# Output projection of a Griffin-style block: five pairs of token tiles as seven block products each

## The chip, the cores and the metric

The kernel runs on one core of one Trainium2 chip. The metric is the device time of one execution in microseconds; the kernel before takes 2026.76 us (median of 3 runs, 2026.57 to 2026.84).

A core has five engines that run side by side, each with a queue of its own: TensorE (PE, matmul; its weight loads are shown apart as PEld), VectorE (DVE), ScalarE (ACT), GpSimd (POOL) and SyncE (SP), which here only issues DMA transfers. An engine takes its instructions in the order of its queue. An instruction that must wait holds back those behind it.

## The reference

One encoder layer over 2048 tokens of 1024 channels, all float32. Two attention branches, a and b, each give 512 channels per token; a gated merge and an output projection with a residual follow:

```python
merged = gate_a * (ya @ w_branch_a[layer]) + gate_b * (yb @ w_branch_b[layer])
h = h + merged @ w_out[layer]          # 2048x1024 @ 1024x1024
return rms_norm(h, final_norm_gain)    # each row divided by the root of its mean square, times a gain
```

The change is in the last two lines: the product with `w_out`, the sum with x, and the norm of each row.

## The kernel before

**Precision.** TensorE takes operands in a rounded float32 form. So each operand is kept as a high part (a rounded copy, made by ACT) and a low part (the rest: the value minus its high part, by DVE or POOL). This is called a split. A product of two operands is three matmuls: high x high, high x low, low x high (`mm3`, L225, and `product`, L1544).

**The stage ahead.** The attention of both branches is one long interleaved sequence. It writes the b branch's last result `y_of("b", 3)` late. `branch(m, G, c)` (L1081) multiplies a branch's result for 512 tokens (group G) with one of eight column blocks c of `w_branch`: it loads the weights (tag `dst`), splits them on ACT and POOL into the tile `dw` (L1087, L1088; one place for each), does 12 matmuls into the PSUM tile `d` (one place), multiplies by the gate on DVE (L1094, gate from tag `sig`), adds the other branch's part on POOL (L1101) and writes to `mD` in HBM. `mD[g]` is the merged result of 512 tokens, transposed: 128 x 8 blocks of channels x 512 tokens. When the last stage begins, only the eight `branch("b", 3, c)` are missing; they feed token tiles 12 to 15.

**The last stage** (L1519 to L1603) works on 16 token tiles of 128 rows. Their number is t. `load_m` (L1163) brings the merged result of a pair of tiles as four loads of 256 KB (tag `mf`) and splits each on ACT (L1170) and POOL (L1171) into one tile of `wp_` (tags P0 and P1 in turn). The eight weight blocks of 128 rows of `w_out` stand split on chip as `ws[k]`: blocks 0 to 4 (`wosh`, `wosl`, `wosy`) are prepared during attention, blocks 5 to 7 (`wos`) after its buffers are closed (L1145, L1146). Per tile and half of the 1024 output columns, `product` makes 8 x 3 matmuls of 128 tokens x 512 columns into one of four PSUM banks. DVE adds the row of x (L1594), ACT squares and sums (L1595). After both halves DVE takes the reciprocal root by whole-number arithmetic and three Newton steps in one column (`rsqrt`, L136 to L150) and multiplies by root and gain (L1602); SP writes the row out (L1603). Tile 15 (`last`) does the same with its last half cut in two.

**The order.** The kernel is written with a tile framework. It puts each engine's instructions into an order by a planner that runs a timeline of its own at compile time; waits are put in from the tiles' reads and writes. In the stage before the change the planner orders all engines: matmuls of `branch` stand between the matmuls of the tiles wherever its timeline found them ready. `tc.manual_schedule` takes an engine out of the planner's hands: that engine's instructions then stand in the order in which the program names them. A tile with a tag shares its place in memory with others of the tag, and its first writer waits until the readers of the one before are done.

## Time and profile before

| what | value |
|---|---|
| median of 3 runs | 2026.76 us |
| the profiled execution | 2026.53 us |
| its span | 2024.7 us |
| TensorE busy over the span | 1966.8 us (97%) |
| DVE, ACT, POOL busy over the span | 1446.5, 1268.4, 810.4 us |
| TensorE busy from 1840 to 1906 us | 65.99 of 66 us |
| TensorE busy from 1929 to 2011 us | 82.00 of 82 us |

The last stage takes the final 190 us of the span, from some matmuls before 1832 us that fill holes of the attention to the last row's way out. The lines of the profile name the engine, the line of the kernel, the operation, the tile it writes and the tiles it reads (`po<-wos,mm` writes the PSUM tile po from wos and mm), and in brackets how long the engine was idle before and what it waited for. A matmul's duration in the trace is its latency; matmuls overlap, so what one costs is the spacing of their starts.

### The profile page before, as it was taken

The page shows a single profiled execution, that of the slowest core. Times are in us where ns is not written, and L with a number is a line of the kernel's source. Part 1 is how long each engine was busy: PE and PEld are TensorE (multiplying, and loading weights), DVE is VectorE, ACT ScalarE, POOL GpSimd, SP SyncE. Part 2 cuts the span into 40 slices and gives each one's busy share as a digit, 9 for nine tenths or more (in the row PEclk, how much of TensorE's full clock was granted, in tenths as well). Part 3 has the DMA queues.
Part 4 walks back from the last instruction along what each step waited for, and adds up shares of the span by engine and source line. Part 5 has one row for each costly group of instructions (what it writes and reads, how often), then busy time and mean ns, then how long its engine had stood idle before and what let it go on. Part 6 is the DMA issues. An engine that isn't in the chain of part 4 may idle for free. (4 is left out here: it accounts for less than half of the span.)

```text
span 2024.7 us, 34050 instructions
## 1 busy us (share of the span) xinstructions
PE 1966.8 (97%) x10677; PEld 1685.8 (83%) x10677; DVE 1446.5 (71%) x3584; ACT 1268.4 (63%) x2539; POOL 810.4 (40%) x1057
## 2 busy tenths in 40 slices
PE   8999999999999999999989999999999999999998
PEld 7788888889889888778768888888988898887886
DVE  6737778797989988665556778658876688765444
ACT  6446666566576645355487879758986698773221
POOL 2232233321172454554335564563445444442420
PEclk9999999999999999999999999999999999999999
DMA  9573444565465665478998565574346531325632
GB/s 352 195 238 107 144 145 144 159 187 159 155 212 161 210 221 178 129 243 276 290 285 276 177 209 153 167 236 124 120 154 201 180 101 53 110 89 182 224 135 94
DMA packets 244730, 363.16 MB, mean 179 GB/s; under 512 B 31168, under 2 KB 115776, under 8 KB 244416
## 3 DMA queue, kind: packets, MB, share of 16 engines
q1 hardware_dynamic: 244544, 360.94, 55.4%
q8 instruction: 85, 1.39, 0.3%
q14 instruction: 101, 0.83, 0.1%
HBM read 244.23 MB, written 116.62 MB: 178 GB/s over the span
## 5 line engine op out<-in xcount | busy, mean ns | idle before, releaser
L225 PE MATMUL acc<-xh,wt 128*128 128x512 f32 x2128 | 676.6, 392 | 4.6 <-DVE keepikT L1476 1.3
L225 PEld LDWEIGHTS acc<-xh,wt 128*128 128x128 f32 x2128 | 399.4, 188 | 90.2 <-DVE wt L1291 1.9
L225 PE MATMUL acc<-xl,wt 128*128 128x512 f32 x1064 | 415.5, 391 | 0.1
L861 POOL TENSOR_TENSOR ptl<-pf,pth 128x512 fp32r<-128x512 f32 (+1 forms) x144 | 179.8, 1249 | 223.3 <-ACT pf L857 171.1
L225 PEld LDWEIGHTS acc<-xl,wt 128*128 128x128 f32 x1064 | 200.3, 188 | 41.2 <-DVE xl L1284 0.4
L864 DVE TENSOR_TENSOR ptl<-pt,pth 128x512 fp32r<-128x512 f32 (+1 forms) x288 | 187.1, 659 | 44.5 <-ACT pth L863 43.7
L515 DVE SCALAR_TENSOR_TENSOR sc<-lg,iw,sc 128x512 f32<-128x512 f32 (+2 forms) x266 | 178.7, 678 | 52.1 <-ACT lg L510 46.8
L216 POOL TENSOR_TENSOR wt<-wst,wt 128x512 fp32r<-128x512 f32 (+1 forms) x96 | 117.3, 1249 | 233.3 <-ACT wt L215 205.6
L1024 PE MATMUL s<-kBt,qsB 128*128 128x512 f32 (+3 forms) x640 | 188.8, 386 | 5.7 <-DVE mx L840 3.1
L510 ACT ACTIVATE lg<-lg 128x512 f32<-128x512 f32 (+2 forms) x304 | 150.2, 526 | 48.6 <-PE lg L508 47.5
L863 ACT ACTIVATE pth<-pt 128x512 fp32r<-128x512 f32 (+1 forms) x288 | 159.9, 579 | 33.1 <-PE pt L1041 16.7
L1027 ACT ACTIVATE P<-P,mx 128x128 f32<-128x128 f32 (+15 forms) x128 | 154.6, 1210 | 22.4 <-DVE mx L840 21.8
L1041 PE MATMUL pt<-ident,P 128*128 128x128 f32 x1088 | 166.6, 273 | 1.9 <-DVE ptl L864 0.8
L1049 PE MATMUL O<-pth,vBt 128*128 128x256 f32 x544 | 147.9, 290 | 3.5 <-ACT pth L863 1.5
L1049 PE MATMUL O<-ptl,vBt 128*128 128x256 f32 x544 | 147.3, 297 | 2.7 <-POOL ptl L861 1.3
L840 DVE CUSTOM_DVE_ANT_0 P<-s,mk,mx 128x512 f32<-128x512 f32 (+2 forms) x192 | 125.2, 652 | 29.4 <-PE s L1024 21.0
L1041 PEld LDWEIGHTS pt<-ident,P 128*128 128x128 f32 x1088 | 126.4, 140 | 11.3 <-DVE ptl L864 2.0
L1088 POOL TENSOR_TENSOR dw<-dst,dw 128x512 fp32r<-128x512 f32 x64 | 82.5, 1291 | 106.3 <-ACT dw L1087 99.5
L1024 PEld LDWEIGHTS s<-kBt,qsB 128*128 128x128 f32 x640 | 103.7, 192 | 18.7 <-DVE mx L840 9.7
L563 ACT ACTIVATE jk<-sc,st 128x640 int8<-128x640 f32 (+6 forms) x49 | 71.2, 1453 | 70.0 <-DVE st L581 60.4
L1049 PEld LDWEIGHTS O<-ptl,vBt 128*128 128x128 f32 x544 | 102.6, 189 | 12.8 <-DVE ptl L864 6.5
L914 PE MATMUL s<-kk,qz 128*128 128x256 f32 (+1 forms) x448 | 106.9, 334 | 5.5 <-DVE mx L840 5.2
(320 smaller groups left out, 4449.0 us busy)
## 6 DMA issues: line engine op xcount, KB each, us to landing
wst<-wP SPq DMA_DIRECT2D x80, 256.0 KB
wst<-wS SPq DMA_DIRECT2D x72, 256.0 KB
kk<-kA SPq DMA_DIRECT2D x56, 256.0 KB
vs<-vA SPq DMA_DIRECT2D x56, 256.0 KB
wst<-wS SPq DMA_DIRECT2D x72, 192.0 KB
qz<-qA SPq DMA_DIRECT2D x96, 128.0 KB
qD<-q SPq DMA_DIRECT2D x39, 256.0 KB
part<-qD SPq DMA_DIRECT2D x39, 256.0 KB
```

The costliest lines, as they stand in the source:

```text
L216: nc.gpsimd.tensor_tensor(wt[:, 1, k:k + n, c * 128:(c + 1) * 128], st, f32(hi), op=OP.subtract)
L225: m = nc.tensor.matmul(acc, a, b, start=(first and i == 0), stop=(last and i == n - 1), **({} if first and last else {"skip_group_check": ...
L510: nc.scalar.activation(lg, lg, AF.Relu)
L515: nc.vector.scalar_tensor_tensor(o_, lg, wv, o_, op0=OP.mult, op1=OP.add)
L840: nc.vector.tensor_tensor_reduce(dst, ps_, add, 1.0, FMAX if first else mx, OP.add, OP.min, accum_out=mx)
L861: nc.gpsimd.tensor_tensor(lo, pf, f32(hi), op=OP.subtract)
L863: nc.scalar.activation(hi, src, AF.Copy)
L864: nc.vector.tensor_tensor(lo, src, f32(hi), op=OP.subtract)
L1024: nc.tensor.matmul(s_ps[:, :w], q[:, h, :], kBt[:, m, a:a + w], start=(m == 0), stop=(m == 1))
L1027: nc.scalar.activation(P[:, e, :n], P[:, e, :n], AF.Exp, bias=mx[:, e:e + 1], scale=-1.0, accum_out=st["sum"][:, (u % 2) * 2 + e:(u % 2) * ...
L1041: nc.tensor.transpose(pt[:, k, e, :], P[:, e, (kt + k) * 128:(kt + k + 1) * 128], ident)
L1049: nc.tensor.matmul(o_, vBt[:, kt + k, :], src[:, k, :], start=(kt + k == 0 and n_ == 0), stop=(kt + k == b and n_ == 1), skip_group_check= ...
```

## The change

Tiles 0 to 5 (`FIRST7 = 6`) go as before. Tiles 6 to 15 go in five pairs. The operand of a pair is 256 tokens x 1024 channels. It is cut into four blocks A11, A12 (first tile, first and second half of the channels), A21, A22 (second tile); `w_out` into B11, B12, B21, B22 of 512 x 512. The 2 x 2 block product, eight block products of four k-steps, is now made with seven (Winograd's form of Strassen's method):

- operands, per pair: S1 = A21 + A22, S2 = S1 - A11, S3 = A11 - A21, S4 = A12 - S2;
- weights, once: T1 = B12 - B11, T2 = B22 - T1, T3 = B22 - B12, T4 = B21 - T2;
- products: A11 B11, A12 B21, S1 T1, S2 T2, S3 T3, A22 T4, S4 B22, put together by accumulating in PSUM and by additions on DVE and POOL with the rows of x.

The parts of the edit:

- Order: TensorE's queue in this stage is in the program's order. It begins with blocks 5 and 6 for the four half rows of tiles 0 and 1, then block 7; the eight `branch` products follow one per half row, from the second half of tile 1 to the first half of tile 5. Block 5 and 7 are staged over the tag `sig` (block 7 waits for block 5), no longer `dst`.
- `sums_of_weights(k)` after tiles 1 to 4, `last_sum_of_weights(k)` after tile 5: 12 and 4 loads of 256 KB, sums on POOL, splits on ACT and DVE. The first are held by a small copy on POOL from a value of the tile before. T4 lies in the places of the b branch's result (tags `yb0`, `yb1`), free after the last `branch`.
- `blocks(t)` loads a pair's operands (A1 in the place `dw`, 512 KB; A12 and A22 in `sig`), makes the four sums and seven splits; the splits of the next pair lie in a ring of eight places (P0, P1), and each is issued behind the product that frees its place.
- `seven(t, n, then)` is a pair; `close_pair` takes the roots of both rows at once, with its small values in a PSUM tile. The last pair makes A22 T4 in a bank of its own ahead of A12 B21, closes row 15 on POOL and ACT, and ends with tile 14's second half cut in two as before (`close_last`).

```diff
         for k in range(WK, KT):
             load_w(k, one_=wo.tile([128, 2, D], F32R, name=f"wos{k}"),
-                   tags=((("sig", 2), ("sig", 2)), (("dt", 2), ("dt", 2)), (("dst", 1), ("dst", 1)))[(KT - 1 - k) % 3])
+                   tags=((("sig", 2), ("sig", 2)), (("dt", 2), ("dt", 2)), (("sig", 2), ("sig", 2)))[k - WK])
...
+        def sums_of_weights(k, gate):
...
+            st = [ld.tile([128, 512], F32, name="tst", tag=g_, bufs=n) for g_, n in (("bias", 2), ("bias", 2), ("sg", SGB))]
+            for z, (k_, hf) in zip(st, ((k, 0), (k, 1), (k + 4, 1))):
+                nc.gpsimd.tensor_copy(z[:, 0:1], gate)
+                nc.sync.dma_start(z, io["wO"][:, k_, hf * 512:hf * 512 + 512])
+            nc.gpsimd.tensor_tensor(st[0], st[1], st[0], op=OP.subtract)
+            nc.gpsimd.tensor_tensor(st[1], st[2], st[1], op=OP.subtract)
+            nc.gpsimd.tensor_tensor(st[2], st[2], st[0], op=OP.subtract)
+            for j, z in ((1, st[0]), (3, st[1]), (2, st[2])):
+                nc.scalar.activation(twh[j][:, k], z, AF.Copy)
+                nc.vector.tensor_tensor(twl[j][:, k], z, f32(twh[j][:, k]), op=OP.subtract)
+
+        def last_sum_of_weights(k):
...
+            nc.sync.dma_start(z, io["wO"][:, k + 4, 0:512])
+            nc.gpsimd.tensor_tensor(z, z, f32(twh[2][:, k]), op=OP.subtract)
+            nc.gpsimd.tensor_tensor(z, z, f32(twl[2][:, k]), op=OP.subtract)
+            nc.scalar.activation(twh[4][:, k], z, AF.Copy)
+            nc.vector.tensor_tensor(twl[4][:, k], z, f32(twh[4][:, k]), op=OP.subtract)
+
+        def blocks(t):
...
+            A1 = dn.tile([128, 4, 256], F32, name="a1", tag="dw", bufs=1)
+            nc.sync.dma_start(A1, mD[g, :, 0:4, o:o + 256])
+            f = {"A11": A1[:, :, 0:128], "A21": A1[:, :, 128:256]}
+            for i in range(2):
+                f[f"A{i + 1}2"] = dn.tile([128, 4, 128], F32, name="a2", tag="sig")
+                nc.sync.dma_start(f[f"A{i + 1}2"], mD[g, :, 4:8, o + i * 128:o + i * 128 + 128])
...
+            def split(n_, e):
+                r_ = (rot("ring", 8) + 4) % 8
...
+                hi, lo = (ring[r_ // 4][:, r_ % 4, z] for z in range(2))
+                nc.scalar.activation(hi, f[n_], AF.Copy)
+                e.tensor_tensor(lo, f[n_], f32(hi), op=OP.subtract)
+                ops[t][n_] = hi, lo
+
+            split("A11", nc.vector)
+            for n_, tag, e, a, b, op in (("S1", "dt", nc.gpsimd, "A21", "A22", OP.add), ("S2", "dt", nc.vector, "S1", "A11", OP.subtract),
+                                         ("S3", "ta", nc.gpsimd, "A11", "A21", OP.subtract), ("S4", "ta", nc.vector, "A12", "S2", OP.subtract)):
...
+            for n_, e in (("S2", nc.vector), ("S1", nc.gpsimd), ("S3", nc.gpsimd), ("A12", nc.gpsimd), ("A22", nc.vector), ("S4", nc.gpsimd)):
+                yield
+                split(n_, e)
...
+        def close_pair(t, hs, ss):
+            z = psd.tile([128, 512], F32, name="rz", tag="d", bufs=1)
+            v, w, a = (z[:, 4 * i:4 * i + 2] for i in range(3))
...
+            for _ in range(NEWTON):
+                nc.vector.tensor_tensor(a, v, y, op=OP.mult)
+                nc.vector.tensor_tensor(a, a, y, op=OP.mult)
+                nc.vector.scalar_tensor_tensor(y, a, 1.5, y, op0=OP.add, op1=OP.mult)
+            for i in range(2):
+                for hf in range(2):
...
+                    nc.vector.scalar_tensor_tensor(hs[i][:, n_], hs[i][:, n_], y[:, i:i + 1], g2[:, n_], op0=OP.mult, op1=OP.mult)
+                nc.sync.dma_start(out[(t + i) * 128:(t + i + 1) * 128, :], hs[i])
+
+        def seven(t, n, then):
...
+            def times(acc, n_, w, first, last_):
+                block_product(acc, m[n_], w, first, last_)
+                if then:
+                    next(then, None)
...
+            times(a, "A11", bw(0, 0), True, False)
+            nc.scalar.activation(p1, a, AF.Copy)
+            nc.gpsimd.tensor_tensor(q12, p1, x0[:, v], op=OP.add)
+            nc.gpsimd.tensor_tensor(q22, p1, x1[:, v], op=OP.add)
+            nc.gpsimd.tensor_tensor(q21, p1, x1[:, u], op=OP.add)
+            times(b, "S2", tw(2), True, False)
+            nc.vector.tensor_tensor(q12, b, q12, op=OP.add)
+            times(c, "S1", tw(1), True, False)
+            times(b, "S3", tw(3), False, end)
+            nc.vector.tensor_tensor(q22, b, q22, op=OP.add)
+            nc.vector.tensor_tensor(h1[:, v], c, q22, op=OP.add)
...
+            times(a, "A12", bw(1, 0), False, True)
+            nc.vector.tensor_tensor(h0[:, u], a, x0[:, u], op=OP.add)
...
+            times(b, "A22", tw(4), False, True)
+            nc.vector.tensor_tensor(h1[:, u], b, q21, op=OP.add)
...
+            times(c, "S4", bw(1, 1), False, True)
+            nc.vector.tensor_tensor(h0[:, v], c, q12, op=OP.add)
...
+        ph.enter_context(tc.manual_schedule(engines={mybir.EngineType.PE}))
+        for t in range(2):
+            for hf in range(2):
+                product(t, hf, WK, KT - 1)
         load_r(0)
...
+        load_m(2)
+        c = 0
+        for t in range(FIRST7):
+            load_r(t + 1)
+            if t == 2:
+                load_m(4)
             for hf in range(2):
...
+                half_row(t, hf)
+                if (t > 1 or t and hf) and c < 8:
+                    branch("b", NG - 1, c)
+                    c += 1
+            if 1 <= t < 5:
+                sums_of_weights(t - 1, rows_[t - 1][1][:, 0:1])
+        for k in range(4):
+            last_sum_of_weights(k)
+        first = blocks(FIRST7)
+        for _ in first:
+            pass
+        load_r(FIRST7 + 1)
+        for n, t in enumerate(range(FIRST7, NT, 2)):
+            seven(t, n, blocks(t + 2) if t + 2 < NT else None)
...
```

More of the change, by code (lines that the diff above doesn't have):

```diff
@@ L63 @@
 FADE = 0.8
+FIRST7 = 6
 WIDE = 0.8
@@ L1531, in load_r, with cols_of, product @@
             nc.sync.dma_start(xrs[t], x[t * 128:(t + 1) * 128, :])
-        def product(t, hf, k0, k1, parts=1):
+        def cols_of(k, hf):
+            return tuple(w[:, hf * 512:hf * 512 + 512] for w in ws[k])
+        def product(t, hf, k0, k1):
             m, o = mts[t - t % 2], t % 2 * 128
@@ L1539, in product @@
                 mh, ml = (m[:, z, k, o:o + 128] for z in range(2))
-                pieces = parts if k == KT - 1 else 1
-                w_ = 512 // pieces
-                for c in range(0, 512, w_):
-                    for i, (a, b) in enumerate(((mh, ws[k][0]), (mh, ws[k][1]), (ml, ws[k][0]))):
-                        nc.tensor.matmul(accs[t, hf][:, c:c + w_], a, b[:, hf * 512 + c:hf * 512 + c + w_],
-                                         start=(k == 0 and i == 0), stop=(k == KT - 1 and i == 2 and c + w_ == 512))
@@ L1547, in last @@
-        def last(t):
-            xt = xrs.pop(t)
-            hh = hp.tile([128, D], F32, name="hh", tag="hh")
-            hg = hp.tile([128, 512], F32, name="hg", tag="hg", bufs=1)
-            ss = hp.tile([128, 3], F32, name="ss3", tag="ss3", bufs=1)
-            v = hp.tile([128, 1], F32, name="vr", tag="vr")
-            product(t, 0, 0, KT)
-            nc.vector.tensor_tensor(hh[:, 0:512], accs.pop((t, 0)), xt[:, 0:512], op=OP.add)
-            nc.scalar.activation(xt[:, 0:512], hh[:, 0:512], AF.Square, accum_out=ss[:, 0:1])
+                wh, wl = cols_of(k, hf)
@@ new lines, in product @@
+                for i, (a, b) in enumerate(((mh, wh), (mh, wl), (ml, wh))):
+                    nc.tensor.matmul(accs[t, hf], a, b, start=(k == 0 and i == 0), stop=(k == KT - 1 and i == 2))
+        twh, twl = {}, {}
+        def sums_of_weights(k, gate):
+            if not twh:
+                for j in (1, 2, 3):
+                    tw = sums.tile([128, 2, 4, 512], F32R, name=f"tw{j}")
+                    twh[j], twl[j] = tw[:, 0], tw[:, 1]
+            st = [ld.tile([128, 512], F32, name="tst", tag=g_, bufs=n) for g_, n in (("bias", 2), ("bias", 2), ("sg", SGB))]
[8 more added lines that the diff above has]
+                nc.vector.tensor_tensor(twl[j][:, k], z, f32(twh[j][:, k]), op=OP.subtract)
@@ new lines, in last_sum_of_weights @@
+        def last_sum_of_weights(k):
+            if 4 not in twh:
+                twh[4], twl[4] = (dn.tile([128, 4, 512], F32R, name=f"tw4{z}", tag=f"yb{z}", bufs=1) for z in range(2))
+            z = ld.tile([128, 512], F32, name="tst", tag=("bias", "bias", "sg", "bias")[k], bufs=(2, 2, SGB, 2)[k])
+            nc.sync.dma_start(z, io["wO"][:, k + 4, 0:512])
[3 more added lines that the diff above has]
+            nc.vector.tensor_tensor(twl[4][:, k], z, f32(twh[4][:, k]), op=OP.subtract)
@@ new lines, in block_product @@
+        def block_product(acc, a, w, first, last, parts=1):
+            ah, al = a
+            for k in range(4):
+                wh, wl = w(k)
+                w_ = 512 // (parts if k == 3 else 1)
+                for c in range(0, 512, w_):
+                    for i, (l_, r_) in enumerate(((ah, wh), (ah, wl), (al, wh))):
+                        nc.tensor.matmul(acc[:, c:c + w_], l_[:, k], r_[:, c:c + w_], start=(first and k == 0 and i == 0),
+                                         stop=(last and k == 3 and i == 2 and c + w_ == 512), skip_group_check=True)
@@ L1556, in last, with close_last @@
+        def close_last(t, hh, ss, acc, q, m):
+            v = hp.tile([128, 1], F32, name="vr", tag="vr")
+            hg = dn.tile([128, 512], F32, name="hg", tag="dt")
+            junk = dn.tile([128, 512], F32, name="junk", tag="dt")
             nc.vector.tensor_tensor(hg, hh[:, 0:512], g2[:, 0:512], op=OP.mult)
             nc.vector.tensor_scalar(v, ss[:, 0:1], 1.0 / D, EPS, op0=OP.mult, op1=OP.add)
-            product(t, 1, 0, KT, 2)
-            acc = accs.pop((t, 1))
+            block_product(acc, m, bw(1, 1), False, True, 2)
@@ L1571, in last, with half_row @@
                 nc.sync.dma_start(out[t * 128:(t + 1) * 128, n_], hh[:, n_])
+        rows_ = {}
+        def half_row(t, hf):
+            if hf == 0:
+                rows_[t] = hp.tile([128, D], F32, name="hh", tag="hh"), hp.tile([128, 3], F32, name="ss3", tag="ss30")
+            hh, ss = rows_[t]
+            n_ = slice(hf * 512, hf * 512 + 512)
+            product(t, hf, KT - 1 if t < 2 else 0, KT)
+            nc.vector.tensor_tensor(hh[:, n_], accs.pop((t, hf)), xrs[t][:, n_], op=OP.add)
+            nc.scalar.activation(xrs[t][:, n_], hh[:, n_], AF.Square, accum_out=ss[:, hf:hf + 1])
+            if hf:
+                xrs.pop(t)
+                close_row(t, hh, ss)
         for t in range(2):
```

105 lines of the change are left out of this document (76 added, 29 removed).

## The prediction

> **What bounds the kernel now.** I read the busy times by window first, to find the engine that is full in the stage that changes; then TensorE's order of time there; then the groups by operation and shape from 1750 us to the end, for prices; last the order of time of VectorE (DVE) and GpSimd (POOL), where two engines meet.
>
> Windows (length; busy us and instructions of PE, weight loads, DVE, ACT, POOL; granted clock, DMA share, GB/s):
>
> ```profile
> span 2024.7 us, 34050 instructions
> ...
> 1840.00:1906.00 66.00, 65.99 (x291) 54.35 (x290) 34.18 (x91) 16.58 (x36) 28.14 (x22) 1.00 0.67 215
> 1860.00:1880.00 20.00, 20.00 (x90) 16.57 (x89) 12.57 (x28) 4.47 (x10) 10.31 (x8) 1.00 0.78 251
> 1929.00:2011.00 82.00, 82.00 (x364) 67.89 (x363) 37.29 (x120) 17.44 (x42) 15.25 (x12) 1.00 0.35 122
> ```
>
> From 1840 us on TensorE has no idle time, at a granted clock of 1.00, while POOL works 28.14 of 66 us and then 15.25 of 82. The stage is a count of matmuls times their spacing, until something else is late. TensorE in order of time (start, us):
>
> ```profile
> 1832.44 4.76 PE L1544 MATMUL po<-wos,mm 128*128 128x512 f32 x18 [0.17 <-ACT wos L1145]
> 1837.59 0.50 PE L1544 MATMUL po<-wosh,mm 128*128 128x512 f32 x1 [0.39 <-DVE hh L1594]
> ...
> 1943.44 2.20 PE L1544 MATMUL po<-wos,mm 128*128 128x512 f32 x9
> ...
> 1948.88 2.20 PE L1544 MATMUL po<-wos,mm 128*128 128x512 f32 x9
> ```
>
> The same nine matmuls come back after 1948.88 - 1943.44 = 5.44 us: one half row of a token tile, 8 blocks of K times 3 partial products, 24 matmuls. One costs 5.44 / 24 = 0.2267 us.
>
> **What is removed.** Token tiles 6 to 15 go in five pairs. A pair was 2 x 2 x 24 = 96 matmuls; now it is seven products of 4 x 3 = 12 matmuls of the same shape, 84. Five pairs save 60 matmuls, 60 x 0.2267 = 13.6 us. The profiled execution took 2026.53 us (1.8 more than its span; the median of the runs is 0.23 above it). With nothing late: 2026.53 - 13.6 = 2012.9 us. The rest is what will be late.
>
> **Prices** (count, busy us, mean ns):
>
> ```profile
> L1171 POOL TENSOR_TENSOR mm<-mf,mm 128x512 fp32r<-128x512 f32 x28 | 36.0, 1296 | 75.9 <-ACT mm L1170 75.9
> L1602 DVE SCALAR_TENSOR_TENSOR hh<-hh,rs2y,g 128x512 f32<-128x512 f32 x30 | 21.2, 748 | 0.5
> L1594 DVE TENSOR_TENSOR hh<-po,xr 128x512 f32<-128x512 f32 x30 | 20.6, 689 | 58.8 <-PE po L1544 57.4 <-issue 1.2 <-DMA mD<-dt 0.2
> L1170 ACT ACTIVATE mm<-mf 128x512 fp32r<-128x512 f32 x32 | 19.5, 629 | 59.8 <-DMA mf<-mD 45.8 <-issue 8.0 <-PE po L1544 6.0
> L1595 ACT ACTIVATION_READ_ACCUMULATOR xr<-hh 128x1 f32 x30 | 5.6, 187 | 0.0
> L150 DVE SCALAR_TENSOR_TENSOR rs2y<-rs2a,rs2y 128x1 f32<-128x1 f32 x48 | 9.7, 201 | 1.6
> ```
>
> A 128x512 operation is 1.30 us on POOL, 0.69 to 0.75 on DVE, 0.63 on ACT; a square with its sum 0.82; a one-column DVE step 0.2. A load behind another, and the use of a tile in pieces:
>
> ```profile
> 1952.96 0.33 SPq L1531 DMA_DIRECT2D xr<-x  x1
> 1953.38 1.44 SPq L1169 DMA_DIRECT2D mf<-mD  x2
> 1957.66 1.26 ACT L1170 ACTIVATE mm<-mf 128x512 fp32r<-128x512 f32 x2 [4.72 <-DMA mf<-mD]
> ...
> 1871.41 1.30 POOL L1171 TENSOR_TENSOR mm<-mf,mm 128x512 fp32r<-128x512 f32 x1 [1.96 <-ACT mm L1170]
> 1871.73 0.39 PE L1544 MATMUL po<-wosh,mm 128*128 128x512 f32 x1
> ```
>
> A 256 KB load issued at 1953.38 behind 512 KB of x is used at 1957.66: 4.3 us. TensorE reads tile 4's first blocks at 1871.73 while POOL writes its last piece until 1872.71: places in one tile are followed singly.
>
> **The shared wait.** DVE and POOL in order of time:
>
> ```profile
> 1860.27 1.29 POOL L1171 TENSOR_TENSOR mm<-mf,mm 128x512 fp32r<-128x512 f32 x1 [6.56 <-ACT mm L1170]
> 1861.51 1.28 POOL L1101 TENSOR_TENSOR dt<-ta,dt 128x512 f32<-128x512 f32 x1
> 1862.75 1.29 POOL L1088 TENSOR_TENSOR dw<-dst,dw 128x512 fp32r<-128x512 f32 x1
> ```
>
> ```profile
> 1860.31 1.26 DVE L146 SCALAR_TENSOR_TENSOR rs2a<-rs2y,vr 128x1 f32<-128x1 f32 x1
> 1861.60 1.21 DVE L150 SCALAR_TENSOR_TENSOR rs2y<-rs2a,rs2y 128x1 f32<-128x1 f32 x1
> 1862.85 1.21 DVE L146 SCALAR_TENSOR_TENSOR rs2a<-rs2y,vr 128x1 f32<-128x1 f32 x1
> 1864.09 0.16 DVE L150 SCALAR_TENSOR_TENSOR rs2y<-rs2a,rs2y 128x1 f32<-128x1 f32 x1
> ```
>
> The one-column DVE step with two inputs in SBUF, 0.16 us when POOL is idle (1864.09), ends each time just as a POOL operation ends. POOL keeps its 1.24 us spacing. So a DVE instruction with two SBUF inputs waits out the POOL instruction in progress, and the change gives POOL more to do.
>
> **A pair in the steady state.** TensorE needs 84 x 0.2267 = 19.0 us. POOL: sums S1 and S3, four splits, three additions of the first product to the residual, 9 x 1.30 = 11.7. ACT: seven splits and a copy, 8 x 0.63, and four squares, 4 x 0.82, 8.3. DVE: three splits, two sums, six additions, 11 x 0.69; four closing products, 3.0; the pair's root, 14 x 0.2: 13.4. Nine of those DVE operations have two SBUF inputs; with POOL busy 11.7 / 19.0 = 0.62 of the time and half an operation left on average, they wait 9 x 0.62 x 0.65 = 3.6 more: 17.0 of 19.0. Loads are seven issues a pair (A1, two A2, two rows of x, two of out) against eight, with the same 3 MB. No engine is full, so no cost in throughput. But DVE must add S2's product to the residual while S1's runs (2.7 us), before S3 goes into the same bank, behind the four closing products of the pair before. I take 0.3 us a pair, 1.5; bounds 0 (always in time) and one POOL operation per pair, 5 x 1.3 = 6.5.
>
> **The part ahead of the pairs.** TensorE's order is now written by hand. The first wait, 0.17, stays; the 0.39 on the accumulator goes, since blocks 5 and 6 of all four half rows come first; block 7's staging now waits for block 5's split, 4.3 + 0.63 + 0.69 after about 1833, 1838.6, where its first use is at 1832.4 + 24 x 0.2267 = 1837.9. These cancel: 0, bounds -0.6 and +2. The eight products of branch b then stand one per half row (5.44 us), each needing ACT 0.63 and POOL 1.30 after the one before leaves the place: 1.9 us, 4.5 with two POOL operations ahead. Covered; 0.5, bounds 0 and 4 (half of them 1 us late). POOL's work there: branches 16 operations, one load of tiles 4, 5: 4, weight sums 12 and then 8: 40 x 1.30 = 52 us in 1905.9 - 1837.9 = 68. The sums (20 operations on POOL, 16 each on ACT and DVE, 16 loads in SP's queue at 0.33 us an issue) cost nothing as long as these 68 us of matmuls cover them; without cover each POOL operation in excess costs 1.3. The loads added, 16 x 256 KB = 4 MB over 68 us, are 60 GB/s on top of rows of 215 to 251 GB/s at a DMA share of 0.67 to 0.78; I price them in the bounds.
>
> **The first pair.** Its start without delays is 1832.4 + (36 + 192 + 96) x 0.2267 = 1905.9 (blocks 5 to 7 of tiles 0 and 1, tiles 2 to 5, eight branch products). A1 takes the place of the last branch's weights, free 24 matmuls earlier, 1900.4. Load 4.3, ACT 0.63, DVE 0.69, some 0.4 between: 6.0 against 5.44 of cover, 0.6 late. A22 takes a place that DVE frees after the last branch's product, 0.8 later; then S1 on POOL 1.30, S2 on DVE 0.69, split 0.63 + 0.69: ready 1900.4 + 0.8 + 4.3 + 3.3 + 0.4 = 1909.2, wanted at 1906.5 + 2.7 = 1909.2; two waits behind POOL, up to 1.3 each, come on top. POOL has the weight sums' rest in its queue too. I take 2.0 in all; bounds 0 and 6. What is queued behind: on ACT and DVE the later splits, on TensorE everything.
>
> **The end.** The last pair's order (A22 ahead of A12) closes row 15 under 24 matmuls, 5.4 us, and the last product and its tail keep the form they had: 0, bounds -0.2 and +1.
>
> Sum: 2026.53 - 13.6 + 0 + 0.5 + 2.0 + 1.5 + 0 = 2016.9; with 0.23 to the median, 2017.2 us.
>
> The Trainium skill ("SBUF — State Buffer", sections "SBUF: two separate sides" and "Who interferes with whom") says that GpSimd and a VectorE instruction with two SBUF inputs exclude each other for the whole instruction, whichever starts first. The rows at 1860 to 1864 agree for DVE behind POOL; the one-column steps there cost POOL nothing. By the rule a sum in which both kinds simply add would stand; it is the second rival.
>
> **Rivals.**
> 1. Forecast, 0.62: 2013 to 2020.5.
> 2. The common port fills. From 1837.9 to the A22 product of the first pair (1905.9 + 13.6 = 1919.5) lie 81.6 us. POOL has 40 + 6 (first pair's operands) + 3 = 49 operations, 63.7 us. DVE with two inputs: 16 weight splits, 5 for the operands, 12 closing products, 33 x 0.72 = 23.8, and six roots of seven small steps, 8.4. Added up 95.9, 14.3 too much: 2026.76 - 13.6 + 14.3 = 2027.5, no change. Against it: the small steps cost POOL nothing (87.5 are left, 5.9 too much), and not all must be done by then. Steadily 9 x 1.30 + 9 x 0.72 = 18.2 fits in 19.0. From 9.6 to 17.6 us of delay: 0.07. A part of it, 2020.5 to 2022.8: 0.16.
> 3. Slower: POOL sits on its own loads. The weight sums' loads are held by a small POOL copy until a row is closed; if POOL's queue has the subtraction right behind the copy, POOL waits 4.3 us, and behind it stands the next branch's split, without which TensorE stands too, since its order can't bend. Four sums of weights x 4.3 = 17.2, with the 4.0 already in the sum: 2026.76 - 13.6 + 21.2 = 2034. It decides from 17.6 us of delay in all. For it: the windows' DMA share. Against it, the waits of POOL from 1830 us on (us, times, longest):
>
> ```profile
> POOL dw L1088 <- DMA mD<-dt: 4.0, 1, 4.0
> ...
> POOL dt L1101 <- DMA ta<-tD: 1.0, 2, 0.6
> ```
>
> Before, the queue's order left only these 5.0 us on loads. 0.07.
> 4. It doesn't do what it says: the splits of the next pair wait for whole tiles, so each of 28 products waits for ACT and POOL, 1.9 x 28 = 53: 2066. The piecewise use at 1871.73 speaks against it: 0.02.
> 5. All waits vanish, at 2012.0 to 2013: 0.06.
>
> **Numbers.** Under 2022.8 (faster by over 0.2%, 4 us, about what can be told from no change): 0.62 + 0.16 + 0.06 = 0.84. Within: 0.07. Slower: 0.09. Range 2012.7 to 2023.0.
>
> **What would show it.** Right: seven products spaced 2.72 us, TensorE's pair at 19.0 us, a gap of some 2 us near 1906, the last matmul some 10 us earlier, the tail after it as before. Wrong: idle time of TensorE ahead of branch products with POOL as releaser (rival 3); DVE additions of b late in each pair (steady state); POOL above 0.9 busy from 1840 to 1920 (rival 2). The forecast falls if pairs take 20 us or more, or if the start of the first pair is past 1910.

## The result, and the profile after

The changed kernel takes 2051.36 us (median of 4 runs, 2047.57 to 2053.67) beside 2026.8 us of the kernel before. The ratio is 1.0118, 95% interval 1.0100 to 1.0136: 24 us slower, where 9.6 us faster was forecast. The profiled execution took 2047.57 us, its span is 2045.8 us.

The attention ahead of the last stage ends at a different time in each profiled execution (first matmul of weight block 5 between 1830.6 and 1836.8 us wherever the attention's code is unchanged), and the kernel before spread from 2022 to 2034 us in its runs. So I compare the **last stage**: from that matmul (`po<-wos,mm`, the one with a wait of 0.16 to 0.18 us) to the end of the span. Before it took 2024.7 - 1832.44 = 192.3 us. After, TensorE in order of time (start, us, engine, line, operation, count, idle before and releaser):

```profile
core 0 of [0], span 2045.8 us
...
1830.62 0.51 PE L1547 MATMUL po<-wos,mm 128*128 128x512 f32 x1 [0.16 <-ACT wos L1146]
...
1840.65 2.88 PE L226 MATMUL d<-yb,dw 128*128 128x512 f32 x12
...
1869.31 2.58 PE L226 MATMUL d<-yb,dw 128*128 128x512 f32 x10 [2.78 <-POOL dw L1089]
...
1896.93 3.39 PE L226 MATMUL d<-yb,dw 128*128 128x512 f32 x10 [2.83 <-POOL dw L1089]
...
1917.11 0.50 PE L1618 MATMUL po<-wosh,ring 128*128 128x512 f32 x1 [2.38 <-ACT ring L1598]
...
1926.39 8.15 PE L1618 MATMUL po<-tw,ring 128*128 128x512 f32 x22 [3.36 <-DVE ring L1599]
...
1937.09 3.01 PE L1618 MATMUL po<-tw,ring 128*128 128x512 f32 x12 [2.55 <-DVE px L1691]
...
1948.10 0.39 PE L1618 MATMUL po<-wosh,ring 128*128 128x512 f32 x1
...
1967.57 0.39 PE L1618 MATMUL po<-wosh,ring 128*128 128x512 f32 x1
...
1978.95 4.28 PE L1618 MATMUL po<-tw,ring 128*128 128x512 f32 x12 [3.06 <-DVE rz L1651]
...
1992.38 0.39 PE L1618 MATMUL po<-wosh,ring 128*128 128x512 f32 x1
...
2013.98 0.39 PE L1618 MATMUL po<-wosh,ring 128*128 128x512 f32 x1
...
2024.28 7.33 PE L1618 MATMUL po<-tw,ring 128*128 128x512 f32 x24 [1.98 <-DVE px L1691]
```

The rows at 1917.11, 1948.10, 1967.57, 1992.38 and 2013.98 are the first matmuls of the five pairs. Against matmuls at 0.2267 us each:

| part of the last stage | needs | took | late |
|---|---|---|---|
| up to the first pair, 324 matmuls | 73.5 | 86.5 | 13.0 |
| first pair, 84 matmuls | 19.0 | 31.0 | 12.0 |
| three pairs | 57.1 | 65.9 | 8.8 |
| last pair and the end | 29.1 (as in experiment 15; 27.9 in experiment 3) | 31.8 | 2.7 |
| sum | | 215.2 | 36.5 |

192.3 - 13.6 + 36.5 = 215.2: the 60 matmuls are gone, and nearly three times what they saved is lost, in waits and in matmuls at a lower clock. Of the 13.0 us up to the first pair 1.9 are lost with blocks 5 to 7 (36 matmuls in 10.0 us, from 1830.62 to 1840.65, where 8.2 are needed; the kernel before lost 1.1 in its first 18) and 2.5 in waiting for the first operand of the first pair. Most of the rest stands at two branch products, where TensorE waits for GpSimd's split of the branch weights (dw). In the pairs it waits for VectorE. The busy times by window (us and instructions of PE, weight loads, DVE, ACT, POOL; clock, DMA share, GB/s):

```profile
1860.00:1880.00 20.00, 17.22 (x76) 13.92 (x75) 11.92 (x20) 4.79 (x10) 14.18 (x14) 1.00 0.83 277
...
1900.00:1920.00 20.00, 17.04 (x68) 13.23 (x68) 14.81 (x20) 4.64 (x9) 13.29 (x11) 0.93 0.55 175
1920.00:1940.00 20.00, 14.09 (x44) 10.61 (x43) 19.65 (x23) 6.78 (x14) 17.66 (x13) 0.77 0.33 109
```

From 1860 to 1880 POOL works 14.18 of 20 us where it worked 10.31 before. In the first pair DVE is full (19.65, its waits behind POOL within an instruction included) and the granted clock falls to 0.77. What POOL does ahead of the second late split:

```profile
1892.58 1.29 POOL L1562 TENSOR_TENSOR tst<-tst 128x512 f32<-128x512 f32 x1 [2.89 <-DMA tst<-wO]
1893.94 1.27 POOL L1563 TENSOR_TENSOR tst<-tst 128x512 f32<-128x512 f32 x1
1895.16 1.71 POOL L1089 TENSOR_TENSOR dw<-dst,dw 128x512 fp32r<-128x512 f32 x1
```

Two sums of weights stand ahead of the split, and here POOL has even stood 2.89 us on their load: rival 3 for once. DVE in the first pair and in the last one, and then POOL in the last one:

```profile
1924.59 1.75 DVE L1599 TENSOR_TENSOR ring<-s,ring 128x512 fp32r<-128x512 f32 x1
1926.26 1.23 DVE L1629 TENSOR_TENSOR vr<-ss 128x1 f32<-128x1 f32 x1
...
1934.42 1.41 DVE L1637 SCALAR_TENSOR_TENSOR hh<-hh,rs2y,g 128x512 f32<-128x512 f32 x2
...
1936.36 0.68 DVE L1691 TENSOR_TENSOR px<-po,px 128x512 f32<-128x512 f32 x1
...
2018.32 5.21 DVE L1657 SCALAR_TENSOR_TENSOR hh<-hh,rr,g 128x512 f32<-128x512 f32 x4
2023.45 0.68 DVE L1691 TENSOR_TENSOR px<-po,px 128x512 f32<-128x512 f32 x1
```

```profile
2018.89 1.74 POOL L1688 TENSOR_TENSOR px<-p,xr 128x512 f32<-128x512 f32 x1
2020.59 1.73 POOL L1689 TENSOR_TENSOR px<-p,xr 128x512 f32<-128x512 f32 x1
```

In the last pair the four closings (0.75 us each before) take 5.21 us while POOL adds, POOL's additions 1.74 instead of 1.30, and the addition of b (S2's product, out of the PSUM bank that S3 needs), which TensorE waits for, stands behind them. In the first pair tile 5's root (1926.26 to 1934.4) and two closings stand ahead of it. The third pair, 5.8 of the 8.8 us of the three, is different. First POOL, then DVE:

```profile
1971.79 1.29 POOL L1606 TENSOR_TENSOR s<-a,a 128x512 f32<-128x512 f32 x1 [3.64 <-DMA a<-mD]
```

```profile
1973.11 0.69 DVE L1606 TENSOR_TENSOR s<-s,a 128x512 f32<-128x512 f32 x1 [4.54 <-POOL s L1606]
...
1979.31 6.83 DVE L1657 SCALAR_TENSOR_TENSOR hh<-hh,rr,g 128x512 f32<-128x512 f32 x4
```

Here the closings come after the addition of b (1978.11 to 1978.80; TensorE goes on at 1978.95). Ahead of it DVE stands 4.54 us on S1 of the next pair, and POOL, which makes S1, 3.64 us on the load of a block.

### The profile page after: what moved, and what is told of

Its sections match the earlier page's. It is cut to its first block, busy times and chain, and to the rows that moved or that the text cites. A ratio compares the mean times of both kernels' runs of the same rounds, so it can differ in the third digit from the quotient of the medians.

```text
span 2045.8 us, 34170 instructions
## 1 busy us (share of the span) xinstructions
PE 1963.8 (96%) x10617; PEld 1678.9 (82%) x10617; DVE 1508.3 (74%) x3602; ACT 1290.8 (63%) x2577; POOL 889.3 (43%) x1116
## 5 line engine op out<-in xcount | busy, mean ns | idle before, releaser
L1050 PEld LDWEIGHTS O<-pth,vBt 128*128 128x128 f32 x544 | 102.9, 189 | 12.4 <-ACT pth L864 3.5
```

The source lines that it names most:

```text
L1050: nc.tensor.matmul(o_, vBt[:, kt + k, :], src[:, k, :], start=(kt + k == 0 and n_ == 0), stop=(kt + k == b and n_ == 1), skip_group_check= ...
```

## The experiments

Theories. **A**: DVE instructions with two SBUF inputs and POOL instructions hold each other up, far more than the forecast's 0.4 us each, and what stands behind them in a queue is late. **B**: TensorE's order by hand can't bend and costs the time. **C**: DVE, or DVE and POOL together, have too little time whatever the order. **D**: loads are late, and POOL or ACT stands on them. All runs (median; ratio to the kernel before run beside it, with its 95% interval; last stage of the one profiled execution, so one sample for each). The diffs are shortened, and what stands behind # explains them.

| run | us | ratio | last stage |
|---|---|---|---|
| before | 2026.8 | | 192.3 |
| after | 2051.36 | 1.0118 (1.0100 to 1.0136) | 215.2 |
| 1 order by hand alone | 2029.13 | 1.0010 (0.9999 to 1.0021) | 192.3 |
| 2 closings on ACT | 2040.61 | 1.0070 (1.0047 to 1.0093) | 207.2 |
| 3 additions from PSUM | 2039.83 | 1.0071 (1.0047 to 1.0095) | 204.3 |
| 5 DVE by hand | 2048.96 | 1.0114 (1.0097 to 1.0130) | 211.4 |
| 6 three pairs | 2045.92 | 1.0108 (1.0091 to 1.0125) | 212.5 |
| 7 = 5 and 3 | 2041.92 | 1.0077 (1.0057 to 1.0097) | 206.0 |
| 8 = 7 and 6 | 2046.34 | 1.0101 (1.0084 to 1.0117) | 208.1 |
| 9 no sums of weights | 2038.38 | 1.0059 (1.0043 to 1.0076) | 201.9 |
| 10 = 7 and 9 | 2024.97 | 0.9988 (0.9979 to 0.9998) | 188.9 |
| 11 = 10, A1 early | 2027.71 | 1.0002 (0.9992 to 1.0012) | 193.8 |
| 12 = 7, sums on DVE, A1 early | 2038.84 | 1.0062 (1.0045 to 1.0079) | 204.6 |
| 13 = 7, loads of the sums only | 2029.11 | 1.0003 (0.9993 to 1.0014) | 190.7 |
| 14 = 7, subtractions only | 2046.44 | 1.0074 (1.0050 to 1.0098) | 207.7 |
| 15 sums in the attention | 2034.73 | 1.0038 (1.0023 to 1.0052) | 189.7 |
| 16 = 15, operands early | 2038.26 | 1.0049 (1.0033 to 1.0065) | 193.3 |
| 17 = 15, held back | 2028.13 | 1.0007 (0.9998 to 1.0016) | 190.3 |
| 18 = 17, farther apart | 2028.8 | 1.0006 (0.9997 to 1.0015) | 188.2 |

**1. Order by hand alone.** All 16 tiles plain, TensorE in the program's order:

```diff
-        for t in range(FIRST7):
+        for t in range(NT):          # tiles 6 to 15 as 0 to 5; no sums_of_weights, blocks, seven
```

> Only the order of the changed kernel: TensorE's queue of the last stage stands in the program's order, with one branch product per half row, and the staging of weight blocks 5 to 7 as changed. All 16 token tiles go as 96 matmuls a pair, with no weight sums and no block products, and tile 15 ends as in the kernel before. Theory port (VectorE instructions with two SBUF inputs and GpSimd instructions exclude each other, and the added GpSimd work makes VectorE late): GpSimd's work is that of before, so the time is within 3 us of before, 2025 to 2030. Rival order (an order by hand can't bend round a late operand): the 9 us that TensorE lost between the first weight blocks and tile 6 in the changed kernel mostly stay, 2033 to 2037.

The stage takes 192.3 us as before. B falls as a cause by itself. Whether an order by the planner would have put other matmuls into the waits of the changed kernel was not run.

**4. The disputed cost by itself.** A small program on blocks in SBUF and PSUM: POOL alone, DVE alone, both.

```diff
+    for i in range(pool_n):
+        nc.gpsimd.tensor_tensor(po_, a, b, op=OP.add)
+    for i in range(dve_n):
+        nc.vector.tensor_tensor(vo_, a, b, op=OP.add)      # two inputs in SBUF
+        # or (vo_, p, b): p in PSUM; or a[:, 0:2], b[:, 0:2]
```

> Only a measurement, none of the layer is computed: 12 additions of 128x512 on GpSimd alone; 12 on VectorE alone, once with both inputs in SBUF and once with one in PSUM; then 12 on GpSimd beside 24 on VectorE with two SBUF inputs, beside 24 with one input in PSUM, and beside 40 of two columns with two SBUF inputs. Theory port: beside two SBUF inputs the two streams add up, 12 x 1.29 + 24 x 0.69 = 32 us, or VectorE finishes late by about GpSimd's time; beside PSUM they overlap, 24 x 0.69 = 17 us; the short ones end with GpSimd's instructions, one or two per 1.29 us. Rival (no common port): all overlap, 17 us, and the short ones take 40 x 0.2 = 8 us.

POOL: alone, beside 24 DVE additions from SBUF, beside 24 from PSUM, beside 40 short ones; then DVE in the last three:

```profile
8.37 15.99 POOL L44 TENSOR_TENSOR po<-a,b 128x512 f32<-128x512 f32 x12
...
42.94 20.05 POOL L44 TENSOR_TENSOR po<-a,b 128x512 f32<-128x512 f32 x12 [1.89 <-ACT a L33]
...
72.31 16.03 POOL L44 TENSOR_TENSOR po<-a,b 128x512 f32<-128x512 f32 x12 [7.29 <-ACT a L33]
...
90.51 16.00 POOL L44 TENSOR_TENSOR po<-a,b 128x512 f32<-128x512 f32 x12 [0.41 <-ACT a L33]
```

```profile
42.82 27.95 DVE L49 TENSOR_TENSOR vo<-a,b 128x512 f32<-128x512 f32 x23 [0.62 <-ACT a L33]
...
71.42 17.36 DVE L51 TENSOR_TENSOR vo<-p,b 128x512 f32<-128x512 f32 x24
...
90.39 19.55 DVE L53 TENSOR_TENSOR vo<-a,b 128x2 f32<-128x2 f32 x40 [0.35 <-ACT a L33]
```

With two SBUF inputs the engines take turns: 20.05 / 12 = 1.67 us for one of each, where POOL alone needs 1.33. So a DVE addition costs 1.67 instead of 0.60 (two DVE starts 0.60 apart without POOL), and slows POOL too. With one input in PSUM neither feels the other. Two-column additions cost POOL nothing (16.00), but while it runs they take 1.11 us each in the median, and some 23 of the 40 get through beside its 12. Both prices stand in the kernel's own rows above too (1.75, 1.74).

**2 and 3. Take DVE's closings away; take POOL's additions away.** 2 closes on ScalarE, without the gain; 3 leaves nothing out and gives DVE three more additions a pair:

```diff
-  nc.vector.scalar_tensor_tensor(hs[i][:, n_], hs[i][:, n_], y[:, i:i + 1], g2[:, n_], ...)
+  nc.scalar.activation(hs[i][:, n_], hs[i][:, n_], AF.Copy, scale=y[:, i:i + 1])          # 2
```
```diff
-  nc.scalar.activation(p1, a, AF.Copy)
-  nc.gpsimd.tensor_tensor(q12, p1, x0[:, v], op=OP.add)      # and q22, q21
+  nc.vector.tensor_tensor(q12, a, x0[:, v], op=OP.add)       # 3
```

> The changed kernel with the four closing products of a pair taken from VectorE: ScalarE multiplies each half row by its root (the multiplication by the gain is left out there). Theory port and queue (the closings stand ahead of the additions of b in VectorE's queue and take 5 to 7 us there, behind GpSimd, instead of 2.8): TensorE's waits for the additions in pairs 10, 12 and 14, some 8 to 12 us with the lower clock after them, mostly go: 2037 to 2043. Rival loads (the next pair's sums wait for late operands and hold VectorE's queue): 2046 to 2051.

> The changed kernel with the three additions of the first product to the rows of x moved from GpSimd to VectorE, which reads the product from PSUM: per pair 3 operations less on GpSimd and one copy less on ScalarE, 3 more (one SBUF input each, 0.69 us) on VectorE. Theory port: GpSimd holds the common port 3.9 us less a pair, the 2.1 us more on VectorE wait for nobody: faster than the changed kernel, 2036 to 2045. Rival throughput (VectorE has simply too much to do): 2.1 us a pair more on it, 2051 to 2058.

Each gives some 11 us (8.0 and 10.9 of them in the last stage). With 2 the three middle pairs are 1.0 us late together instead of 8.8, so what the late load did in the third pair goes too when the closings go; whether they made that load late was not followed. The first pair is 2.8 us later. With 3 the middle pairs are 6.1 us late, the first pair gains 3.0 and the end 3.9. That 3 gains although DVE has more to do speaks against C: what counts is rather how long POOL is in DVE's way, and what stands behind.

**5 to 8. DVE's queue by hand; fewer pairs.** In 5 the closings of a pair stand behind the next pair's addition of S2's product and the next operands' work behind h1 (rows of h in x's places). 6 begins the pairs at tile 10, with the sums of weights after the branch products. 7 is 5 with 3; 8 is 7 with 6.

```diff
+        ph.enter_context(tc.manual_schedule(engines={PE, DVE}))       # 5, 7, 8: from the pairs on
             nc.vector.tensor_tensor(q12, b, q12, op=OP.add)
+            for f_ in owed: f_()                                      # closings of the pair before
-            close_pair(t, hs, ss)
+            owed.append(lambda: close_pair(t, hs, ss))
-FIRST7 = 6
+FIRST7 = 10                                                           # 6, 8
```

> The changed kernel with VectorE's queue in the last stage written by hand too: the closing products of a pair (and of tile 5) stand behind the next pair's addition of S2's product, the next pair's operand work follows the addition into h's second half, and S4's sum stands right ahead of its split. Rows of h lie in the places of x. GpSimd has the same work; nothing is left out. Theory A (what is short ahead of an addition of b is the time that the four closings beside GpSimd take in an in-order queue): the waits on px in pairs 6, 10, 12 and 14 go (2.6 + 3.6 + 2.0 + 2.0 us and the clock lost with them), time 2036 to 2041; waits on dw ahead of the branch products stay (5.6 us). Theory C' (VectorE and GpSimd together have too little time, whatever the order): the waits move to later operations, time within 4 us of 2051.

> The changed kernel with the pairs beginning at tile 10 instead of 6: three pairs, and the sums of weights after tiles 6 to 8 and 9, so behind the branch products instead of beside them. 36 matmuls are saved instead of 60: 8.2 us instead of 13.6. Nothing is left out. Theory A: the branch products meet the GpSimd work they had before plus nothing, so no wait on dw stands ahead of them (5.6 us and the lower clock behind the second go), the first pair's start is late by 0 to 2.5; the pairs lose as in the changed kernel (pair 1: 12 us, later ones 0.4 to 6): 2035 to 2042. If instead the hand-written order makes the branch products late, waits on dw stay at 5 us or more in this kernel too.

> VectorE's queue by hand as in the first kernel of this call, and the three additions of the first product to x on VectorE, straight from PSUM, instead of ScalarE's copy and GpSimd. GpSimd has 6 operations a pair instead of 9, VectorE 14 additions and sums that read PSUM or two places in SBUF. Nothing is left out. Theory A: both gains where they differ; the additions alone gave 11.5 us, the order is worth some 10 to 13, and part of these is the same wait: 2029 to 2035, with the branch products' 5.6 us and some 3 us in the first pair left. Theory C' : 2038 or more.

> All three: three pairs from tile 10 on, sums of weights behind the branch products, VectorE's queue by hand, additions straight from PSUM. 8.2 us of matmuls are saved. Theory A: no wait on dw, pairs late by under 1 us each, the first pair 1 to 5 us: 2020 to 2026, a little under the kernel before. If the sums of weights cost TensorE time wherever they stand, they now delay plain tiles 6 to 9 and the first pair: 2027 to 2035.

All four lie above the range given for A; 5 and 7 lie in the one given for C (within 4 us of 2051; 2038 or more). C alone doesn't fit the middle pairs, though: 5 halves the lateness of the three middle pairs (4.6 us), not the rest: 15.4 us late to the first pair and 12.3 in it. 7 brings the middle pairs to 2.9 us, a wait of 0.6 to 0.85 in each, but 17.4 us ahead of the pairs (4.4 more than in the changed kernel, which was not followed) and 7.7 in the first one stay. 8 pays in the same places: there the planner put three sums ahead of the last branch split, and TensorE waits 2.17 us for DVE and 2.57 us for that split. 6 shows where the losses belong: the branch products wait only 0.34 + 0.36 us once most of the sums stand behind them, and the first pair pays instead. DVE is still at the roots and closings of the last plain tiles and the sums' splits there, and nearly full (18.41 us busy from 1960 to 1980), so for this stretch C may hold:

```profile
1979.81 5.49 PE L1618 MATMUL po<-tw,ring 128*128 128x512 f32 x12 [17.44 <-DVE px L1691]
```

**9 to 12. Without the sums of weights; other places for the work.** 9 is after, 10 is 7, with loads, subtractions and splits of the sums left out and blocks of `w_out` as operands. 11 is 10 with the first pair's A1 in a place of x rows; for that, rows of h of the plain tiles lie in x's places and their squares in PSUM. 12 leaves nothing out.

```diff
-                sums_of_weights(t - 1, rows_[t - 1][1][:, 0:1])       # 9, 10, 11; and last_sum_of_weights
-            return lambda k: (twh[j][:, k], twl[j][:, k])
+            return bw(j // 2 % 2, j % 2)
-            A1 = dn.tile([128, 4, 256], F32, name="a1", tag="dw", bufs=1)
+            A1 = hp.tile([128, 4, 256], F32, name="a1", tag="xr", bufs=4)   # 11, 12: first pair
-            nc.gpsimd.tensor_tensor(st[0], st[1], st[0], op=OP.subtract)
+            nc.vector.tensor_tensor(st[0], st[1], st[0], op=OP.subtract)    # 12: all 20
```

> The changed kernel without the sums of weights: their loads, subtractions and splits are left out, and the products take blocks of w_out in the place of the sums, so the values differ and the matmuls are the same in number and shape. From the first matmul of block 5 to the start of the second pair the changed kernel takes 117.5 us where its matmuls need 92.5. If the sums of weights, beside the branch products and the first pair, are what costs these 25 us: 8 to 14 are left (operand loads of the first pair, VectorE's order), time 2034 to 2040. If GpSimd's and VectorE's other work fills the shared wait anyway: under 5 us gained, 2045 or more.

> The same left out of the kernel with VectorE's queue by hand and the additions straight from PSUM. There the four later pairs already lose only 3.1 us together and the part up to the second pair 25.0. If both theories hold they add up: 5 to 9 of the 25 left, so the stage takes 187 to 191 us against 192.3 in the kernel before: 2019 to 2026. If the two remedies cure the same wait: 2030 or more.

> As the kernel before it in this call, and the first pair's A1 loads into a place of x rows, free by 1890 us, instead of the last branch product's weights (rows of h of tiles 0 to 5 lie in x's places, squares in the product's bank). If the late place of A1 costs the 4.3 us ahead of the first pair: 3 to 5 us less than that kernel, 2015 to 2022. If the loads are late for another reason (the queue of transfers, A22's place): within 1 us of it.

> Nothing left out: VectorE's queue by hand in the pairs, additions straight from PSUM, A1 early, and the 20 subtractions of the sums of weights on VectorE (0.7 us each) instead of GpSimd (1.3, and the wait of VectorE beside each). If what hurts is GpSimd in front of the branch's splits and on the port: 2022 to 2030, 8 to 14 us less than with the subtractions on GpSimd. If what hurts is the sums' loads and the waits for them in an in-order queue, VectorE now stands on them and TensorE with it: 2034 or more.

The sums cost 215.2 - 201.9 = 13.3 us in the changed kernel and 206.0 - 188.9 = 17.1 with both remedies in place; sums 13.3 and remedies 9.2 alone, 26.3 together, 3.8 more than added up. 11 missed: A1 was there, but TensorE then waited 4.25 us for S2's operand, which needs A22 too (POOL waits 6.21 us for its load). 12 lies in the range of its other theory (2034 or more): with the subtractions on DVE, TensorE waits for DVE, and DVE stands on loads of the sums, for 5.55 us right ahead of S2's sum, which the second of these waits is for:

```profile
1898.99 3.00 PE L226 MATMUL d<-yb,dw 128*128 128x512 f32 x12 [3.36 <-DVE dt L1095]
...
1926.30 1.22 PE L1624 MATMUL po<-tw,ring 128*128 128x512 f32 x2 [7.44 <-ACT ring L1599]
```

**13 and 14. Work or loads?** Both on 7: 13 leaves the subtractions out, 14 the loads (it subtracts blocks that are on chip).

```diff
-            nc.gpsimd.tensor_tensor(st[0], st[1], st[0], op=OP.subtract)    # 13: all 20 left out
-                nc.sync.dma_start(z, io["wO"][:, k_, hf * 512:hf * 512 + 512])    # 14: all 16
+                nc.gpsimd.tensor_tensor(z, f32(h_), f32(l_), op=OP.subtract)
```

> The kernel with VectorE's queue by hand and the additions straight from PSUM, where the sums of weights cost 206.0 - 188.9 = 17.1 us of the last stage. Left out here: the 20 subtractions on GpSimd. The 16 loads, their small copies and the splits on ScalarE and VectorE stay (the loaded blocks are split as they are, so values differ). If GpSimd's work ahead of the branches' splits is the cause: 12 to 16 of the 17 go, 2025 to 2031. If the transfers beside the branches' own loads are (gate loads, operand loads late): under 5 go, 2036 or more.

> The same kernel with the loads left out and the 20 subtractions kept, on blocks of w_out that are on chip already (values differ); the small copies that hold them stay. GpSimd and the port have the same work, but GpSimd never stands on a load of weights and the queue of transfers has 16 issues and 4 MB less. If GpSimd's work as such is the cause: 0 to 4 us gained, 2036 to 2042. If it is GpSimd standing on its own loads, and the loads that come late behind them: 8 or more gained, 2025 to 2034.

The first matmul of block 5 in 13 and then in 14, with two waits of the branch products of 14:

```profile
core 0 of [0], span 2025.2 us
...
1834.50 0.50 PE L1547 MATMUL po<-wos,mm 128*128 128x512 f32 x1 [0.18 <-ACT wos L1146]
```

```profile
core 0 of [0], span 2040.4 us
...
1832.71 0.50 PE L1547 MATMUL po<-wos,mm 128*128 128x512 f32 x1 [0.18 <-ACT wos L1146]
...
1864.94 4.49 PE L226 MATMUL d<-yb,dw 128*128 128x512 f32 x12 [4.20 <-DVE dt L1095]
...
1890.33 2.56 PE L226 MATMUL d<-yb,dw 128*128 128x512 f32 x10 [2.67 <-POOL dw L1089]
```

2025.2 - 1834.50 = 190.7 us, 2040.4 - 1832.71 = 207.7 us. Of the 17.1 us the subtractions are 15.3, loads and splits 1.8; without any load of the sums to stand on, TensorE waits as long for POOL and DVE (14 gains nothing, and is above both ranges given for it). D falls as the main cause; rival 3's stand at 1892 is real, but a part. The wait of 4.20 us in 14 is for DVE, which was making a root, at 1.2 us a step beside POOL, and two closings. What these runs don't separate is how much of the 15.3 us is the subtractions' own time in a queue and how much the engines' holding each other up; 12, with them on DVE, takes nearly as long (204.6), there with waits on loads.

**15 to 18. Is the saving there, with nothing left out?** The sums are made during the attention and lie in HBM; the last stage loads and splits them. Two of the four closings move behind the addition into h1. 16 also gives A1 and A22 free places; 17 and 18 hold the loads with a small POOL copy and place the four groups later.

```diff
+    def early_sums(k):           # 4 loads, 4 subtractions on POOL, 4 stores; 20, 16, 12, 8 units before the last
+            nc.gpsimd.tensor_copy(z[:, 0:1], shared["mx"][:, 0:1])    # 17 (10, 8, 6, 4), 18 (16, 12, 8, 4)
-                nc.sync.dma_start(z, io["wO"][:, k_, hf * 512:hf * 512 + 512])
+                nc.sync.dma_start(z, TD[j - 1, k])
-            close(1, 0); close(1, 1)
+            late.extend(((1, 0, close), (1, 1, close)))               # behind the addition into h1
```

> Nothing left out. The kernel with VectorE's queue by hand and the additions straight from PSUM; the 16 subtractions of the sums of weights are made during the last part of the attention, where GpSimd is 40% busy and the DMA share is 0.3, and written to HBM; the last stage loads the sums (16 loads of 256 KB, as before) and only splits them. Two of a pair's four closings stand behind the addition into h1's second half. The kernel with the loads alone took 190.7 us in the last stage against 192.3 in the kernel before; the closings should take the 0.6 us waits of the later pairs away, 3 us in all: stage 187 to 189. The attention may lose 0 to 4 us by the 32 transfers and 16 operations: 2022 to 2029. If the loss had been the loads' after all, the stage is above 195 and the time above 2031.

> The same with A1 of the first pair in a place of x rows and A22 loaded ahead of A12, so that neither waits for the last branch product: the first pair's waits (5 us in the kernel with the loads alone) should fall to 1 to 2. 2 to 4 us less than the kernel before it in this call: 2019 to 2026. If the operands are late by the queue of transfers, no gain.

> The kernel with the sums of weights made during the attention, which had a last stage of 189.7 us against 192.3 in the kernel before but began it 11 us later: all four groups of loads and subtractions had run between 1595 and 1640 us, GpSimd standing on their loads. Now each group's loads are held by a small GpSimd copy from a value of the attention unit beside it, and the groups go with the units 10, 8, 6 and 4 before the last, where the DMA share is 0.05 to 0.3. If the loss in the attention came from that crowding: the last stage begins 0 to 4 us later than before's, 2023 to 2029. If GpSimd work and loads delay the attention wherever they stand: 2031 or more.

> The same with the groups at the units 16, 12, 8 and 4 before the last, so farther apart. Within 2 us of the kernel before it in this call if the spacing there is enough; 2 to 4 us less if two groups still meet.

S2, S1 and S3 (36 matmuls) of three pairs running in 15:

```profile
1949.75 8.32 PE L1632 MATMUL po<-tw,ring 128*128 128x512 f32 x36
...
1968.79 8.32 PE L1632 MATMUL po<-tw,ring 128*128 128x512 f32 x36
...
1987.83 8.32 PE L1632 MATMUL po<-tw,ring 128*128 128x512 f32 x36
```

They are 19.04 us apart: 84 x 0.2267, nothing late. But 15 missed its time: the stage began at 1843.6 us, TensorE was busy 33.04 us from 1600 to 1640 instead of 39.36, and POOL stood on the loads of the sums there (waits of POOL from 1560 to 1760 us: total, times, longest):

```profile
POOL est L1169 <- DMA est<-wO: 13.0, 5, 5.1
```

Held back, the stage begins at 1835.1 and 1836.4 us and takes 190.3 and 188.2, 2.0 and 4.1 us less than before; the median times don't show that gain. These starts lie within the spread of 1830.6 to 1836.8, so whether the attention loses it or other executions don't have it stays open. No version with nothing left out is faster than the kernel before; 17 and 18 are the same within 0.16%. 16 missed, by a wait for S2's operand:

```profile
1931.74 10.19 PE L1633 MATMUL po<-tw,ring 128*128 128x512 f32 x36 [6.96 <-ACT ring L1608]
```

In its trace ACT stands 6.28 us, to 1927.99, on the load of a sum of weights (L1585), and S2's sum on DVE and its split on ACT stand behind the split of that sum. So loads, a small part in 13, can cost 7 us when one comes late.

## Why the prediction was wrong

- **60 matmuls, 13.6 us: right.** 84 x 0.2267 = 19.04 us is what a pair takes where nothing is late (15).
- **The part ahead of the pairs, 0.5 us (0 to 4): this step failed first.** It added up POOL's work, 52 us in 68, and called it covered. POOL was indeed busy only 56.78 of the 80 us from 1840 to 1920. But the sums need not run out of time to do harm: each branch product depends on one POOL split and one DVE product within 5.4 us, in queues that take the sums in between; "two POOL operations ahead" was in the text, at 1.30 each and with no wait of its own. With the start of the stage (1.9, forecast 0) and of the first pair (2.5) it was 13.0 us late. 9 shows that the sums are the cause (with all of them left out it is 2.2), 13 and 14, on the kernel of 7, that it is the subtractions as work. That 16 loads cost little was right there (1.8 us with their splits).
- **The first pair, 2.0 us (0 to 6): 12.0 us in it alone.** The bounds held load and splits, each once. In the profile three of its four DVE splits meet a POOL operation (up to 1.75 us instead of 0.69), tile 5's root and two closings stand ahead of the addition of b, and TensorE falls to a lower clock: 22 matmuls took 8.15 us (row at 1926.39), some 3 more than at 0.2267 each. Its waits add up to 6.5 of the 12.0 us. Without the subtractions, and with DVE's order and the additions of 7, it is 5.8 us late (13).
- **The shared wait, "9 x 0.62 x 0.65": the mis-sized term.** It took POOL as busy at random and half an operation as the mean wait, 0.4 us. In the pairs the two engines' work falls into the same microseconds (rows at 2018), and there they take turns: 1.67 us for one of each, 1.07 more per DVE instruction and a third of a microsecond more per POOL instruction. So the four closings take 5.2 to 6.8 us instead of 3.0, with POOL beside them for part of the time.
- **A pair in the steady state, 0.3 us (0 to 1.3): 8.8 / 3 = 2.9.** The risk was named rightly, the addition of b "behind the four closing products of the pair before"; it is late by that in the last pair. In the third it is late behind the next pair's S2 sum and a late load, a wait that the sum of terms didn't have: the forecast counted the loads only by number and size. 2 takes both away (1.0 us in three pairs), so the closings are a link of both; so do the order and the additions in 15 (none). "No engine is full" was true there (DVE 47.27 and POOL 38.26 of 65.88 us) and did not matter.
- **The end, 0 (-0.2 to +1).** Of the 2.7 us late, 1.98 are the addition of b in the last pair, the term above; 0.7 are left, or 1.9 against the end of experiment 3.
- **Rivals.** 2 had the right mechanism and the wrong size: it counted full occupancy, and its sign, POOL above 0.9 busy from 1840 to 1920, didn't come (0.71); lateness of single operations decided before that. 3 happened once (2.83 us of TensorE). 4 is wrong: in 15 pairs run with nothing late. None came to 2051, since each was priced alone and the pairs' price stood at 1.5.

The Trainium skill ("SBUF — State Buffer", section "Who interferes with whom") says that a VectorE instruction with two SBUF inputs and a GpSimd instruction that reads SBUF exclude each other, and that one with a PSUM input doesn't. Experiment 4 agrees: 20.05 us against 16.03. The rule was read for the forecast and its price taken too low.

## What to carry to other kernels

Busy shares don't price work on GpSimd: count for each result that TensorE waits for how many instructions stand ahead of it in its queue, at the price that they have beside the other engine (here 1.67 us for a pair of them). Where GpSimd feeds data that VectorE or TensorE wants soon, try to let VectorE read from PSUM instead, even if VectorE gets more to do (11 us here, in 3). A fixed preparation, here 20 subtractions, has to be set against the saving in the place where it stands: with loads and splits it cost 13 to 17 us for 13.6 saved, and moved into the attention it left no gain that the median shows.

## What the runs showed of the hardware that was not expected

Two-column DVE instructions beside POOL cost POOL nothing, but 40 of them took 19.55 us, and while POOL ran they took 0.16 to 1.19 us each, 1.11 in the median; an instruction of a Newton step can then take as long as one on a whole block (1.2 us in the rows of the prediction).

The clock: after a wait of 2.78 us ten matmuls took 2.58 us, after 2.83 us 3.39 (rows at 1869.31 and 1896.93), and after 17.44 us twelve took 5.49 us instead of 3.01. The length of the wait alone doesn't decide it, as 11 shows:

```profile
1860.58 4.14 PE L226 MATMUL d<-yb,dw 128*128 128x512 f32 x10 [1.83 <-POOL dw L1089]
```

After 1.83 us ten matmuls took 4.14 us here, at a granted clock of 0.50 from 1862 to 1864 us, while in 12 twelve took 3.00 us after a wait of 3.36 (row at 1898.99), at a clock of 1.00. The Trainium skill ("TensorE: Matmul & The Clock Gate", "Part 1: The HAM clock gate") puts the clock's fall at an idle window of about 3.4 us; here a wait of 1.83 us sufficed once, and one of 3.36 did not. How many of the 36.5 us are the clock's was not measured by itself.
